# Two of four token sums on GpSimd, the other two a block of weights later, in an encoder layer on one Trainium2 core

## The chip, the cores and the metric

The kernel runs on one core of one Trainium2 chip. The core has TensorE (PE, matrix products into the accumulator memory PSUM; the loading of its weights, PEld, is shown apart), VectorE (DVE), ScalarE (ACT), GpSimd (POOL) and SyncE (SP, which here issues the DMAs), all of them working on the on-chip memory SBUF. Each engine takes its instructions in the order in which they were written and waits on semaphores for what the others produce. The metric is the device time of one execution in microseconds; lower is better.

## The reference

One encoder layer is applied to a prompt of 256 tokens and to a sample of 2048 tokens, all of width 1024, in float32. What matters here is its first step, the projection of the normalised tokens by one wide matrix:

```python
def encoder_layer(x, w_in, rpb, w_fourier, b_fourier, g_pre, g_na, g_f, w_out, g_post):
    h = rms_norm(x, g_pre)
    proj = h @ w_in
    q, k, v, z_a, u_f, z_f = jnp.split(proj, [...], axis=-1)
    y_a = neighbourhood_attention(q, k, v, rpb)
    y_f = fourier_mix(u_f, w_fourier, b_fourier)
    ...
    out = mixed @ w_out
    return x + rms_norm(out, g_post)
```

`w_in` is 1024 x 3072: six parts (q, k, v, z_a, u, z_f) of 512 columns. The attention, the Fourier mixing and the output product follow it in the kernel and are not touched by the change.

## The kernel before

**Products.** Float32 products are made of three products of a narrower kind: each operand is split into a high part and a low part, and `mm3` (lines 159 to 162) adds high x high (L160), and the two mixed products (L161, L162). The high part is a cast, made by ScalarE; the low part is "operand minus high part", made by VectorE. So each operand costs a ScalarE instruction and then a VectorE instruction that reads two SBUF tiles.

**The order of the first stages.** The kernel first makes v and u of the prompt and of part of the sample. Then comes a loop over 16 blocks `b` of 128 columns of weights (z_f, z_a, k, q, four blocks each), which makes these for the prompt's 256 tokens. After it, the function `vu` makes v and u of the first group of the sample's tokens (group 0; the sample's 2048 tokens are taken as two groups of 1024), and a long loop makes the other four parts for the group; then the same is done for group 1.

**Sums of token operands.** For the sample the products of a group are arranged in the manner of Strassen's multiplication: both matrices are cut into 2 x 2 parts, and seven products of sums of parts, the operands `j` = 0 to 6, take the place of eight. The four parts of group 0's tokens, `nq[kh, b]`, are tiles of 128 x 4 x 512 numbers (2048 per partition). They are loaded by `n_load`, scaled by VectorE in `n_scale` (L400), and combined by `n_sum` (L423), in this order:

- sum 0: t3 = (1,1) - (0,1), into a new tile
- sum 1: (0,1) = (0,1) - (0,0), in place
- sum 2: (0,0) = t3 + (0,0), in place
- sum 3: (1,0) = (0,0) - (1,0), in place, with the new (0,0)

`n_first(j)` then splits operand `j`: the cast on ScalarE (L428) and the low part on VectorE (L429). Operands 0 and 1 are the parts (0,0) and (1,0) before the sums; operand 2 is (0,0) after sum 2, operand 3 is (0,1) after sum 1, operand 4 is t3, operand 5 is (1,0) after sum 3.

**The loop over the blocks.** In this part of the program the order on all engines is written out by hand (`manual_schedule`). In the pass for block `b` the kernel issues, in this order: loads by SyncE; `b_raw(b + 2)`, which splits the weights of the block after the next (cast L562 or L565 on ScalarE, low part L563 or L566 on VectorE); a scaling (b = 2 to 7) or a sum (b = 8 to 11); `n_first` of operand 1, 2 or 3 (b = 5, 12, 13); from b = 14 on `op_split`, which splits the weights of group 0's first products (casts L477, low parts L478); then block `b`'s 24 products on TensorE, the evacuation of their PSUM tile by ScalarE (L789) and its store by SyncE (L791, L793).

So VectorE's queue holds, one behind the other: the low part of block 10, sum 0, block 11, sum 1, block 12, sum 2, block 13, sum 3, block 14, operand 2, block 15, operand 3, and then the low parts of the first weights of `vu`. Block `b` needs its low weights with its third product. The first product of `vu` needs the first L478 with its second.

**GpSimd** has nothing to do from the folding of u's weights (L265, in the first 30 us) to the sums of weights `w_sums` (L532), which are called within `vu`.

**The second group** does the same kind of work elsewhere: its operands come back from memory, and `b_split` (L439) splits them; there the low parts of operands 3 and 5 are made by GpSimd already.

## Time and profile before

| what | us |
|---|---|
| median of three runs | 966.51 |
| lowest and highest of them | 965.75, 966.55 |
| the profiled execution | 965.94 |
| its span, first to last instruction | 964.1 |
| TensorE busy in the span | 955.2 |
| VectorE busy | 703.4 |
| ScalarE busy | 496.7 |
| GpSimd busy | 427.0 |

The profile is of one execution. Its span reaches from the first to the last instruction; the rest of the execution's time lies around it. A row of the list in order of time gives the start, the duration, the engine, the line of the kernel, the operation, the tile written and the tiles read, the shape, a count where equal instructions were merged into one row, and in square brackets how long the engine had stood idle before and what released it. A row of the stage table gives a stretch of time, then the busy time of each engine in it with the number of its instructions, the clock that TensorE was granted (1.00 is full speed), and the load of the DMA engines.

### The profile page before, as it was taken

To read this page: it belongs to the slowest core of one execution; us is meant where nothing else is said; L and a number is where in the kernel's file an instruction comes from. 1 tells how busy PE (TensorE), PEld (TensorE's weight loads), DVE (VectorE), ACT (ScalarE), POOL (GpSimd) and SP (SyncE) were. 2 spreads that over 40 slices of the span, in tenths; PEclk is the share of its full clock that TensorE was granted. 3 is DMA by queue.
4 is the path that set the end of the run, shared out by engine and by line. 5 is a ranking of instruction groups with operands and counts; after the bars stand their busy time and mean duration, and the time that the engine had idled before them with its cause. 6 is when DMAs were issued, how large, how long until landed. Compare 5 with 4: busy or idle time off the path is not lost.

```text
span 964.1 us, 16993 instructions
## 1 busy us (share of the span) xinstructions
PE 955.2 (99%) x5743; PEld 799.0 (83%) x5743; DVE 703.4 (73%) x1310; ACT 496.7 (52%) x1077; POOL 427.0 (44%) x400
## 2 busy tenths in 40 slices
PE   9999999999999999999999999999999999999997
PEld 7889988888888888888888889888788887888886
DVE  5768978787876855687877458776765656659997
ACT  5845676423334532233344267677666676644443
POOL 2200002464751202674665043577677686524544
PEclk9999999999999999999999999999999999999999
DMA  8899796557848883499888896598877998979993
GB/s 304 317 354 380 248 348 243 199 203 263 298 185 345 299 347 123 181 362 360 308 294 327 306 335 225 169 285 292 258 235 238 287 285 286 301 253 346 332 353 122
DMA packets 140942, 269.81 MB, mean 280 GB/s; under 512 B 13402, under 2 KB 81840, under 8 KB 137464
## 3 DMA queue, kind: packets, MB, share of 16 engines
q1 hardware_dynamic: 140360, 268.32, 79.8%
q8 instruction: 46, 0.75, 0.3%
q10 hardware_dynamic: 432, 0.39, 0.2%
q14 instruction: 40, 0.33, 0.1%
q0 software_dynamic: 64, 0.02, 0.0%
HBM read 179.00 MB, written 96.81 MB: 286 GB/s over the span
## 4 chain that ended last, share of the span: by engine, by line
PE 96%; DVE 1%; DMA 1%; issue 0%; ACT 0%; DVEq 0%; SPq 0%; ACTq 0%
PE po L1454 20%; PE mm L161 18%; PE mm L160 18%; PE mm L162 18%; PE pv L1543 6%; PE ptb L1527 6%; PE s L1185 4%; PE pab L1022 2%; DMA wr<-wo 1%; PE py L160 1%; DMA gpre<-gpre 0%; PE py L162 0%; PE py L161 0%; PE ppq L1060 0%; PE pz L162 0%
## 5 line engine op out<-in xcount | busy, mean ns | idle before, releaser
L160 PE MATMUL mm<-xh,wa 128*128 128x512 f32 x448 | 174.4, 389 | 0.0
L162 PE MATMUL mm<-xh,wa 128*128 128x512 f32 x448 | 174.3, 389 | 0.0
L161 PE MATMUL mm<-xl,wa 128*128 128x512 f32 x448 | 174.3, 389 | 0.0
L532 POOL TENSOR_TENSOR ws<-wr 128x512 f32<-128x512 f32 x16 | 23.7, 1480 | 221.0 <-DVE vuo L505 123.8
L1219 POOL TENSOR_SCALAR w<-w,m 128x465 f32<-128x465 f32 (+9 forms) x136 | 84.7, 635 | 43.5 <-DVE m L1216 34.0
L162 PEld LDWEIGHTS mm<-xh,wa 128*128 128x128 f32 x448 | 84.1, 188 | 17.6
L160 PEld LDWEIGHTS mm<-xh,wa 128*128 128x128 f32 x448 | 84.1, 188 | 17.6
L161 PEld LDWEIGHTS mm<-xl,wa 128*128 128x128 f32 x448 | 84.1, 188 | 17.4
L1454 PE MATMUL po<-wo,yh 128*128 128x512 f32 x272 | 90.5, 414 | 0.0
L547 DVE TENSOR_TENSOR wa<-wr,wa 128x512 fp32r<-128x512 f32 x60 | 72.8, 1222 | 21.8 <-ACT wa L546 21.3
L1454 PE MATMUL po<-w,yh 128*128 128x512 f32 x280 | 86.8, 391 | 0.0
L1212 ACT ACTIVATE w<-w,m 128x465 f32<-128x465 f32 (+9 forms) x136 | 78.3, 579 | 13.3 <-DVE m L1207 12.9
L1207 DVE CUSTOM_DVE_ANT_1 w<-s,tb 128x465 f32<-128x465 f32 (+8 forms) x124 | 61.2, 531 | 9.8 <-PE s L1185 9.3
L161 PE MATMUL mm<-vl,xh 128*128 128x512 f32 x168 | 65.5, 390 | 0.2 <-DVE vl L478 0.2
L162 PE MATMUL mm<-vh,xl 128*128 128x512 f32 x168 | 65.4, 389 | 0.0
L160 PE MATMUL mm<-vh,xh 128*128 128x512 f32 x168 | 65.4, 389 | 0.0
L585 POOL TENSOR_TENSOR mt<-mt,rmask 128x880 f32<-128x880 f32 (+2 forms) x24 | 50.3, 2110 | 32.2 <-DVE mt L581 25.9
L1454 PEld LDWEIGHTS po<-w,yh 128*128 128x128 f32 x280 | 52.2, 188 | 10.9 <-issue 0.4
L1531 DVE COPY pt<-ptb 120x384 f32<-120x384 f32 (+5 forms) x72 | 40.5, 563 | 27.6 <-PE ptb L1527 27.4
L873 DVE TENSOR_TENSOR f<-u,mm 128x512 f32<-128x512 f32 x64 | 43.5, 679 | 22.3 <-PE mm L162 13.6
L546 ACT CAST wa<-wr 128x512 fp32r<-128x512 f32 x60 | 36.5, 618 | 44.7 <-PE mm L162 18.2
L1527 PE MATMUL ptb<-ident,w 128*120 128x128 f32 (+8 forms) x422 | 58.9, 276 | 0.0
(265 smaller groups left out, 2387.4 us busy)
## 6 DMA issues: line engine op xcount, KB each, us to landing
wr<-wz SPq DMA_DIRECT2D x48, 512.0 KB
vl<-sD SPq DMA_DIRECT2D x20, 512.0 KB
xm<-xm SPq DMA_DIRECT2D x9, 1024.0 KB
oD<-ofs SPq DMA_DIRECT2D x18, 512.0 KB
of<-oD SPq DMA_DIRECT2D x18, 512.0 KB
yr<-yD SPq DMA_DIRECT2D x34, 256.0 KB
zD<-f SPq DMA_DIRECT2D x16, 512.0 KB
xD<-nx SPq DMA_DIRECT2D x14, 512.0 KB
```

What stands on the lines that cost most here:

```text
L160: nc.tensor.matmul(out, lh, rh, start=first, stop=False)
L161: nc.tensor.matmul(out, lh, rl, start=False, stop=False)
L162: nc.tensor.matmul(out, ll, rh, start=False, stop=last)
L547: nc.vector.tensor_tensor(out=o[:, 1], in0=src, in1=o[:, 0].bitcast(F32), op=ALU.subtract)
L585: nc.gpsimd.tensor_tensor(out=o, in0=i, in1=rmask[:, m0:m0 + n].unsqueeze(2).to_broadcast([128, n, 80]), op=ALU.add)
L873: nc.vector.tensor_tensor(out=dst(f, b), in0=src(uu[u]), in1=src(p), op=op)
L1207: nc.vector.tensor_tensor_reduce(out=rows(g["w"][b][:, h, :n], w), in0=rows(g["s"][2 * b + h][:, :nr * sw(w)], sw(w))[:, :, :w], in1=tv, s ...
L1212: nc.scalar.activation(w, w, AF.Exp, bias=m[:, h:h + 1], scale=-1.0, accum_out=m[:, 2 + h:3 + h])
L1219: nc.gpsimd.tensor_scalar(w, w, m[:, 4 + h:5 + h], 1.0, ALU.mult, ALU.mult)
L1454: nc.tensor.matmul(p, (d["l"] if x == 2 else d["h"])[:, c], w(n, int(x == 1), c), start=j == 0, stop=j == 11)
L1527: nc.tensor.transpose(ptb[h][:nk, j * 128:j * 128 + 128], g["w"][b][:, h, c0:c0 + nk], ident)
L1543: nc.tensor.matmul(p[hs, b], g["v"][:nk, v, hs], g["pt"][b][:nk, h, j * 128:j * 128 + 128], start=j == 0, stop=j == len(ch) - 1)
```

## The change

Sums 0 and 3 are computed by GpSimd in place of VectorE. Sum 0 is still issued in block 8; sums 1, 2 and 3 are issued in blocks 10, 11 and 12, and no longer in 9, 10 and 11. Everything else stands in the same order. Semaphore waits between the two engines come with it: sum 1 overwrites a part that sum 0 reads, sum 2 reads t3, sum 3 reads what sum 2 wrote, and the splits of operands 4 and 5 read what GpSimd wrote.

```diff
@@ n_sum @@
         o, i0, i1, op = (("t3", (1, 1), (0, 1), ALU.subtract), ((0, 1), (0, 1), (0, 0), ALU.subtract),
                          ((0, 0), "t3", (0, 0), ALU.add), ((1, 0), (0, 0), (1, 0), ALU.subtract))[x]
-        nc.vector.tensor_tensor(out=nq[o], in0=nq[i0], in1=nq[i1], op=op)
+        (nc.vector if x in (1, 2) else nc.gpsimd).tensor_tensor(out=nq[o], in0=nq[i0], in1=nq[i1], op=op)
@@ the loop over the blocks @@
         if 2 <= b < 8:
             x, y = divmod(b, 2)
             n_scale(None, *divmod(x, 2)[::-1], range(2 * y, 2 * y + 2))
-        elif 8 <= b < 12:
-            n_sum(b - 8)
+        if b in (8, 10, 11, 12):
+            n_sum((8, 10, 11, 12).index(b))
         if b in (5, 12, 13):
             n_first((5, 12, 13).index(b) + 1)
```

## The prediction

> **What bounds the kernel now.** I read the page first (its parts 1 and 4), then the stage table of the stretch that the change touches, then VectorE (DVE), ScalarE (ACT) and the weight loads of TensorE (PEld) in order of time there, and last a place, 200 us later, where GpSimd (POOL) already does a sum of the size that is moved.

> ```profile
> span 964.1 us, 16993 instructions
> PE 955.2 (99%) x5743; PEld 799.0 (83%) x5743; DVE 703.4 (73%) x1310; ACT 496.7 (52%) x1077; POOL 427.0 (44%) x400
> PE 96%; DVE 1%; DMA 1%; issue 0%; ACT 0%; DVEq 0%; SPq 0%; ACTq 0%
> ```

> TensorE is busy 99% of the span and is 96% of the chain that ended last. So the rest of the kernel has nothing to give back: a microsecond that TensorE loses anywhere arrives at the end, and little can be won.

> ```profile
> core 0: us, PE busy (x) PEld busy (x) DVE busy (x) ACT busy (x) POOL busy (x), PEclk, DMA share, GB/s
> 98.60:123.00 24.40, 24.19 (x187) 23.18 (x186) 24.40 (x17) 16.95 (x21) 0.00 (x0) 1.00 0.68 230
> ```

> Here, where the four sums stand, it is different: VectorE is busy 24.40 of 24.40 us, GpSimd not at all. Its list in this stretch has no gap:

> ```profile
> 98.64 1.22 DVE L563 TENSOR_TENSOR wl<-wr,wh 128x1024 fp32r<-128x1024 f32 x1
> 99.78 2.28 DVE L423 TENSOR_TENSOR nt<-nx 128x2048 f32<-128x2048 f32 x1
> 101.98 1.22 DVE L563 TENSOR_TENSOR wl<-wr,wh 128x1024 fp32r<-128x1024 f32 x1
> 103.11 2.28 DVE L423 TENSOR_TENSOR nx<-nx 128x2048 f32<-128x2048 f32 x1
> 105.32 1.22 DVE L566 SCALAR_TENSOR_TENSOR wl<-wr,wh 128x1024 fp32r<-128x1024 f32 x1
> 106.45 2.28 DVE L423 TENSOR_TENSOR nx<-nt,nx 128x2048 f32<-128x2048 f32 x1
> 108.66 1.22 DVE L566 SCALAR_TENSOR_TENSOR wl<-wr,wh 128x1024 fp32r<-128x1024 f32 x1
> 109.79 2.28 DVE L423 TENSOR_TENSOR nx<-nx 128x2048 f32<-128x2048 f32 x1
> 111.99 1.22 DVE L566 SCALAR_TENSOR_TENSOR wl<-wr,wh 128x1024 fp32r<-128x1024 f32 x1
> 113.13 2.28 DVE L429 TENSOR_TENSOR xl<-nx,xh 128x2048 fp32r<-128x2048 f32 x1
> 115.33 1.22 DVE L566 SCALAR_TENSOR_TENSOR wl<-wr,wh 128x1024 fp32r<-128x1024 f32 x1
> 116.47 2.28 DVE L429 TENSOR_TENSOR xl<-nx,xh 128x2048 fp32r<-128x2048 f32 x1
> 118.67 4.62 DVE L478 TENSOR_TENSOR vl<-vr,vh 128x1024 fp32r<-128x1024 f32 x4
> ```

> The rows L563/L566 make the low parts of the weight blocks 10 to 15, the four L423 are the sums, the two L429 the low parts of token operands 2 and 3, L478 the first low part that the group's products need. From start to start a sum takes 2.20 us of this queue (99.78 to 101.98), a weight block 1.14, an L429 2.20.

> ```profile
> 104.73 0.19 PEld L161 LDWEIGHTS mm<-pl,wh 128*128 128x128 f32 x1
> 104.85 0.19 PEld L162 LDWEIGHTS mm<-ph,wl 128*128 128x128 f32 x1
> ...
> 116.25 0.19 PEld L161 LDWEIGHTS mm<-pl,wh 128*128 128x128 f32 x1
> 116.60 0.19 PEld L162 LDWEIGHTS mm<-ph,wl 128*128 128x128 f32 x1 [0.16 <-DVE wl L566]
> ...
> 119.94 0.19 PEld L161 LDWEIGHTS mm<-vl,xh 128*128 128x128 f32 x1 [0.52 <-DVE vl L478]
> ```

> The third product of a block (L162) is the first that reads the low weights. 116.60 is that of block 15, and 104.85 is four blocks earlier, block 11's: 116.25 - 104.73 = 11.52, so a block takes 2.88 us. VectorE is only just late today: TensorE waits 0.16 us for block 15 and 0.52 us for the group's first low part. These 0.7 us are all that taking work off VectorE can win here.

> **The change part by part.** Sums 0 and 3 leave VectorE for GpSimd; sums 1 and 2 stay and go one block later, to blocks 10 and 11; sum 3 is issued in block 12. No DMA is added or moved. Off VectorE's queue: 2 x 2.20 = -4.40 us. What a sum costs on GpSimd, and what it does to VectorE meanwhile, is shown at the second group's operands (L439), of the same 128x2048:

> ```profile
> 309.02 5.47 POOL L439 TENSOR_TENSOR xl<-xl,xh 128x2048 fp32r<-128x2048 f32 x1 [28.28 <-ACT xh L438]
> 318.26 5.14 POOL L439 TENSOR_TENSOR xl<-xl,xh 128x2048 fp32r<-128x2048 f32 x1 [3.77 <-ACT xh L438]
> ```

> ```profile
> 307.65 2.35 DVE L478 TENSOR_TENSOR vl<-vr,vh 128x1024 fp32r<-128x1024 f32 x2
> 309.93 0.68 DVE L873 TENSOR_TENSOR f<-u,mm 128x512 f32<-128x512 f32 x1
> 310.52 6.19 DVE L478 TENSOR_TENSOR vl<-vr,vh 128x1024 fp32r<-128x1024 f32 x2
> 316.63 2.28 DVE L439 TENSOR_TENSOR xl<-xl,xh 128x2048 fp32r<-128x2048 f32 x1
> 318.84 0.68 DVE L873 TENSOR_TENSOR f<-u,mm 128x512 f32<-128x512 f32 x1
> 321.93 3.62 DVE L439 TENSOR_TENSOR xl<-xl,xh 128x2048 fp32r<-128x2048 f32 x1 [2.42 <-ACT xh L438]
> ```

> The pair L478 takes 2.35 us at 307.65 and 6.19 us at 310.52, beside the GpSimd instruction: it got to run at 310.52 + 6.19 - 2.35 = 314.36. The last L439 takes 3.62 instead of 2.28: it ran at 323.27. Both are 0.13 us before GpSimd's end (314.49 and 323.40), and 4.36 us after the end of the VectorE instruction during which GpSimd had started (310.00, 318.91). So GpSimd waits for a running VectorE instruction that reads two SBUF tiles, and then such instructions wait for all of GpSimd's; L873, which reads a PSUM tile, runs through (0.68 both times). Everything in VectorE's list above reads two SBUF tiles. From the next free slot of VectorE's queue (0.08 before the end of the running instruction) the queue stands for 4.44 us per sum.

> [...]

> Now in order of time. Sum 0 needs only the last scaling before 98.64, so GpSimd starts in block 10's low part (98.64 to 99.86) and holds VectorE from 99.78 to 104.22. GpSimd's queue has nothing ahead of it and nothing behind it before 153 us:

> ```profile
> 153.21 1.81 POOL L532 TENSOR_TENSOR ws<-wr 128x512 f32<-128x512 f32 x1 [123.76 <-DVE vuo L505]
> ```

> ```profile
> 99.50 1.04 ACT L562 CAST wh<-wr 128x1024 fp32r<-128x1024 f32 x1
> ...
> 109.09 1.90 ACT L428 CAST xh<-nx 128x2048 fp32r<-128x2048 f32 x1
> ...
> 111.15 1.06 ACT L565 ACTIVATE wh<-wr 128x1024 fp32r<-128x1024 f32 x1
> ```

> Block 11's low part, whose cast ends at 100.54, waits at the head of VectorE's queue and runs 104.22 to 105.44 (now to 103.20). TensorE wants it at 104.85: a first stall of 0.6 us. Then, from 105.36 without a gap: block 12 (to 106.50), sum 1 (to 108.70; it overwrites what sum 0 read, but sum 0 is done), block 13 (109.84), sum 2 (112.04), block 14 (113.18). Sum 3 needs sum 2, so GpSimd asks at about 112.2 and gets its turn after block 14, in time for it: VectorE's next instruction, operand 2's low part, cannot be ready, since its cast (now at 109.09) also needs sum 2 and runs from 112.1 to 114.0. Behind that cast ScalarE's queue slips, with an evacuation of PSUM and block 15's cast (111.15 now, about 114.3 then), which is still ahead of VectorE. VectorE stands from 113.18 to 117.62; then operand 2 (to 119.82), block 15 (to 120.96, ended 121.04). TensorE, 0.6 us late, would want block 15's low part at about 117.0 and gets it at 121.1: a stall of 4.1 us. Operand 3 takes VectorE to 123.16, the first L478 ends at 124.38, and the group's first low-part product starts at 124.42 instead of 119.94. Behind it are the same instructions in the same order on all engines; stores and loads that SyncE issues behind ScalarE's evacuations slip by less than TensorE does.

> The sum: -2 x 2.20 + 2 x 4.44 = **+4.5 us** on VectorE's queue, which sets TensorE's start of the group; the 0.6 and 4.1 us of stall are this same delay as TensorE sees it (4.7, less 0.2 us of the waits there today). Moving sums 1 and 2 back costs nothing by itself: VectorE is just as full. Bounds of the unknown, the cost of a sum on GpSimd here: below, nothing of it stops VectorE, which would win the 0.7 us; above, the longest recorded length, 5.47, counted whole from the free slot, 1.03 more per sum, +6.5 us. I take 4.44, because two separate instances agree on it.

> The profiled execution took 965.94 us, 1.84 around its span, and 0.57 below the median of the three runs, 966.51. Put on the median: 966.5 + 4.5 = **971.0 us**.

> **The rivals.** *The clock falls during the stall.* TensorE's clock goes down when it rests:

> ```profile
> 956.90 0.28 PE L1742 MATMUL pl<-w,yl 128*128 128x128 f32 x1
> ```

> ```profile
> 961.50:962.00 0.50, 0.00 (x0) 0.00 (x0) 0.00 (x0) 0.00 (x0) 0.00 (x0) 0.59 1.03 377
> ```

> The last matmul ends at 957.18; the granted clock, a half at the end, averages 0.59 in that half microsecond, so it fell at about 961.6, after 4.4 us. The stall at block 15 is 4.1, less the last product's run. Close, but short of it. If it fell, block 15's 22 remaining products (0.12 us each, 2.64) would take up to twice as long, less 0.5 us that hide under the wait for L478: +2.1, 973.1 us. [...]

> *VectorE is not held up (the other side).* Were the sums on GpSimd to run beside VectorE's instructions, the queue would be 4.4 us shorter and both waits of today would go: 966.5 - 0.7 = 965.8. It turns on one number: below 2.20 us of blocking per sum the change wins, up to 3.2 us it stays within 0.2%. For it speaks only that GpSimd is free here; the rows at 310.52 and 321.93 are against it.

> *The delay is given back later.* If a later stage waited for DMA, TensorE could start late at no cost, and half or more of it would vanish: 968.5 or less. But TensorE is busy 99% of the span, and its order is fixed.

> **How the numbers follow.** Forecast (both sums block VectorE, clock stays up) 0.76, with its own range 970.0 to 972.0 (0.5 for the runs' spread and 0.25 per sum); clock falls or GpSimd takes its longest, 0.14; given back in part, 0.06; not held up, 0.04. The 8-in-10 range takes in the clock's fall: 969.3 to 973.2. About 0.2% (1.9 us) is what a measurement of this kernel can tell from no change. Slower by more: forecast, clock and half of "given back", 0.93. Within: 0.06. Faster by more: the best case wins only 0.7 us, so 0.01.

> **What would show it.** In the changed profile: two GpSimd rows L423 of about 5.2 us, from about 99 and 112; L563 after 100 and L429 after 114 on VectorE some 4 us too long; the weight loads of L162 waiting for L563 by about 0.6 us and for L566 by about 4; TensorE's busy time in 98.6 to 127.5 short by 4 to 5 us; everything behind shifted alike, with the granted clock at 1.00. The prediction fails if these VectorE rows keep 1.22 and 2.28 us, if sum 3 starts elsewhere, or if the granted clock dips behind 121 us.

## The result, and the profile after

The changed kernel takes 972.39 us (median of six runs, 971.50 to 975.33) beside 966.24 us (965.75 to 966.55) for the kernel before on the same chip. The ratio on record is 1.0069, with a 95% interval of 1.0056 to 1.0083: slower by 5.4 to 8.0 us. 971.0 was forecast.

The profiled execution is the fastest of the six, 971.50 us. Its page begins:

```profile
span 969.7 us, 16997 instructions
...
PE 956.0 (99%) x5743; PEld 800.1 (83%) x5743; DVE 710.0 (73%) x1308; ACT 496.6 (51%) x1077; POOL 439.7 (45%) x402
```

The span is 969.7 - 964.1 = 5.6 us longer. GpSimd has two instructions more and is 12.7 us busier. VectorE has two fewer and is 6.6 us busier all the same. These are the list of GpSimd and then that of VectorE where the sums stand:

```profile
98.47 5.41 POOL L423 TENSOR_TENSOR nt<-nx 128x2048 f32<-128x2048 f32 x1 [68.92 <-DMA wr<-wz]
111.78 5.50 POOL L423 TENSOR_TENSOR nx<-nx 128x2048 f32<-128x2048 f32 x1 [7.89 <-DVE nx L423]
```

```profile
98.17 1.22 DVE L563 TENSOR_TENSOR wl<-wr,wh 128x1024 fp32r<-128x1024 f32 x1
100.10 4.87 DVE L563 TENSOR_TENSOR wl<-wr,wh 128x1024 fp32r<-128x1024 f32 x1 [0.71 <-ACT wh L562]
104.89 1.21 DVE L566 SCALAR_TENSOR_TENSOR wl<-wr,wh 128x1024 fp32r<-128x1024 f32 x1
106.03 2.28 DVE L423 TENSOR_TENSOR nx<-nx 128x2048 f32<-128x2048 f32 x1
108.23 1.21 DVE L566 SCALAR_TENSOR_TENSOR wl<-wr,wh 128x1024 fp32r<-128x1024 f32 x1
109.36 2.28 DVE L423 TENSOR_TENSOR nx<-nt,nx 128x2048 f32<-128x2048 f32 x1
111.57 1.21 DVE L566 SCALAR_TENSOR_TENSOR wl<-wr,wh 128x1024 fp32r<-128x1024 f32 x1
113.62 5.80 DVE L429 TENSOR_TENSOR xl<-nx,xh 128x2048 fp32r<-128x2048 f32 x1 [0.84 <-ACT xh L428]
119.35 1.21 DVE L566 SCALAR_TENSOR_TENSOR wl<-wr,wh 128x1024 fp32r<-128x1024 f32 x1
120.48 2.28 DVE L429 TENSOR_TENSOR xl<-nx,xh 128x2048 fp32r<-128x2048 f32 x1
122.68 2.35 DVE L478 TENSOR_TENSOR vl<-vr,vh 128x1024 fp32r<-128x1024 f32 x2
```

Two of VectorE's instructions are far too long. Block 11's low part (100.10) takes 4.87 us instead of 1.22, and operand 2's (113.62) 5.80 instead of 2.28. They got to run only when GpSimd's sums were ending: the sums end at 103.88 and 117.28, and the two instructions got to run at 100.10 + 4.87 - 1.22 = 103.75 and 113.62 + 5.80 - 2.28 = 117.14, which is 0.13 and 0.14 us before. All others keep their length. This execution reached the first row 0.47 us earlier than the one before did (98.17 against 98.64); counted from there, the first L478 starts 122.68 - 118.67 + 0.47 = 4.48 us later.

What TensorE sees of it, as weight loads and as matmuls, in order of time:

```profile
105.02 0.19 PEld L162 LDWEIGHTS mm<-ph,wl 128*128 128x128 f32 x1 [0.57 <-DVE wl L563]
120.61 0.19 PEld L162 LDWEIGHTS mm<-ph,wl 128*128 128x128 f32 x1 [4.01 <-DVE wl L566]
```

```profile
116.52 0.28 PE L161 MATMUL mm<-pl,wh 128*128 128x256 f32 x1
120.61 0.39 PE L162 MATMUL mm<-ph,wl 128*128 128x256 f32 x1 [3.81 <-DVE wl L566]
...
121.02 0.42 PE L161 MATMUL mm<-pl,wh 128*128 128x256 f32 x1
121.23 0.41 PE L162 MATMUL mm<-ph,wl 128*128 128x256 f32 x1
121.44 0.41 PE L160 MATMUL mm<-ph,wh 128*128 128x256 f32 x1
...
125.07 0.40 PE L161 MATMUL mm<-vl,xh 128*128 128x512 f32 x1
```

Block 11 waits 0.57 us for its low weights, block 15 waits 4.01. The group's first low-part product starts at 125.07, where it was 119.94: 5.13 + 0.47 = 5.60 us later, and so 1.12 us more than VectorE's queue explains. The rows after the rest say why: the products of block 15 follow one another in 0.21 us (121.02, 121.23, 121.44), while those of the blocks before take 0.12. The stage table, whose last columns are the granted clock, the DMA share and GB/s, shows the clock:

```profile
core 0: us, PE busy (x) PEld busy (x) DVE busy (x) ACT busy (x) POOL busy (x), PEclk, DMA share, GB/s
98.60:123.00 24.40, 20.22 (x159) 19.82 (x158) 22.85 (x11) 14.68 (x18) 10.78 (x2) 0.96 0.59 206
117.45:120.86 3.41, 0.25 (x2) 0.25 (x3) 3.41 (x3) 3.41 (x5) 0.00 (x0) 1.00 0.23 77
120.86:124.27 3.41, 3.41 (x18) 3.41 (x18) 3.41 (x3) 0.07 (x1) 0.00 (x0) 0.50 0.00 0
124.50:130.00 5.50, 5.50 (x28) 4.60 (x27) 5.09 (x4) 2.78 (x3) 0.00 (x0) 1.00 0.59 163
```

In the rest itself it is still 1.00, from 120.86 to 124.27 it is 0.50, then 1.00 again. From there to the end nothing is given back: counted from the span's start the shift is 5.13 us at the group's first low-part product and 5.6 at the end. In between, TensorE waits 0.9 us for one tile of VectorE's (L1294) where it waited 0.2 before; why this wait is longer is not shown.

### The profile page after: what moved, and what is told of

Its sections match the earlier page's. It is cut to its first block, busy times and chain, and to the rows that moved or that the text cites. A ratio compares the mean times of both kernels' runs of the same rounds, so it can differ in the third digit from the quotient of the medians.

```text
span 969.7 us, 16997 instructions
## 1 busy us (share of the span) xinstructions
PE 956.0 (99%) x5743; PEld 800.1 (83%) x5743; DVE 710.0 (73%) x1308; ACT 496.6 (51%) x1077; POOL 439.7 (45%) x402
## 4 chain that ended last, share of the span: by engine, by line
PE 96%; DVE 1%; issue 1%; DMA 0%; ACT 0%; DVEq 0%; SPq 0%; ACTq 0%
PE po L1454 20%; PE mm L162 18%; PE mm L161 18%; PE mm L160 18%; PE pv L1543 6%; PE ptb L1527 6%; PE s L1185 4%; PE pab L1022 2%; PE py L160 1%; PE py L162 1%; PE py L161 1%; DVE nx L423 0%; DMA gpre<-gpre 0%; PE ppq L1060 0%; PE pz L161 0%
## 5 line engine op out<-in xcount | busy, mean ns | idle before, releaser
L162 PE MATMUL mm<-xh,wa 128*128 128x512 f32 x448 | 174.3, 389 | 0.0
L161 PE MATMUL mm<-xl,wa 128*128 128x512 f32 x448 | 174.3, 389 | 0.0
L161 PEld LDWEIGHTS mm<-xl,wa 128*128 128x128 f32 x448 | 84.1, 188 | 17.4
L162 PEld LDWEIGHTS mm<-xh,wa 128*128 128x128 f32 x448 | 84.1, 188 | 17.4
L532 POOL TENSOR_TENSOR ws<-wr 128x512 f32<-128x512 f32 x16 | 24.2, 1514 | 138.9 <-DMA wr<-wz 126.3
L162 PE MATMUL mm<-vh,xl 128*128 128x512 f32 x168 | 65.4, 389 | 0.0
L161 PE MATMUL mm<-vl,xh 128*128 128x512 f32 x168 | 65.4, 389 | 0.0
L873 DVE TENSOR_TENSOR f<-u,mm 128x512 f32<-128x512 f32 x64 | 43.5, 679 | 21.9 <-PE mm L162 16.5
```

The source lines that it names most:

```text
L161: nc.tensor.matmul(out, lh, rl, start=False, stop=False)
L162: nc.tensor.matmul(out, ll, rh, start=False, stop=last)
L873: nc.vector.tensor_tensor(out=dst(f, b), in0=src(uu[u]), in1=src(p), op=op)
```

## The experiments

Each ratio, with its interval, is the one on record, against runs of the kernel before on the same chip; it is not the quotient of the two medians, and differs from it by up to 0.0014. Diffs are against the changed kernel unless it is said otherwise. "The first L478" is given relative to the first row of VectorE's list, as above.

**All four sums on VectorE, at the changed places.** This keeps the moves of sums 1, 2 and 3 and takes GpSimd out.

```diff
-        (nc.vector if x in (1, 2) else nc.gpsimd).tensor_tensor(out=nq[o], in0=nq[i0], in1=nq[i1], op=op)
+        nc.vector.tensor_tensor(out=nq[o], in0=nq[i0], in1=nq[i1], op=op)
```

> The four sums stand where the changed kernel has them (blocks 8, 10, 11, 12), but all are made by VectorE. Theory (GpSimd's sums block VectorE): VectorE's queue is as long as before, only in another order; block 15's low part and the first L478 end as before, TensorE waits 0.2 and 0.5 us: 966.2 us, within 0.5. Rival (the later places of the sums, and ScalarE's cast of operand 2 waiting for the late sum 2, make the loss): most of it stays, about 970 us, with VectorE idle in front of L429.

Measured: 966.54 us, ratio 0.9994 (0.9985 to 1.0002). The first L478 is 0.30 us later, and TensorE's waits, in the view of waits (total, times, longest), are small:

```profile
PE mm L162 <- DVE wl L566: 0.3, 1, 0.3
PE mm L161 <- DVE vl L478: 0.2, 1, 0.2
```

So the later places cost nothing that can be measured. The loss comes from the engine that does the sums.

**One sum at a time on GpSimd.** First sum 0 alone:

```diff
-        (nc.vector if x in (1, 2) else nc.gpsimd).tensor_tensor(out=nq[o], in0=nq[i0], in1=nq[i1], op=op)
+        (nc.vector if x else nc.gpsimd).tensor_tensor(out=nq[o], in0=nq[i0], in1=nq[i1], op=op)
```

> Sum 0 alone on GpSimd, in block 8; sums 1 to 3 on VectorE in blocks 10 to 12. Theory: one sum off VectorE (-2.20), one block of 4.44: the first L478 2.2 us later; TensorE waits 0.6 us for block 11 and about 1.8 for block 15, too short for the clock to fall: 966.2 + 2.2 = 968.5 us, granted clock as before. Rival (any sum on GpSimd is free unless something waits for its result): 964 to 966.5, since sum 0's result is wanted only three blocks later. Rival (the clock falls in any stall): 969.5 or more, clock under 0.999.

Then sum 3 alone:

```diff
-        (nc.vector if x in (1, 2) else nc.gpsimd).tensor_tensor(out=nq[o], in0=nq[i0], in1=nq[i1], op=op)
+        (nc.vector if x < 3 else nc.gpsimd).tensor_tensor(out=nq[o], in0=nq[i0], in1=nq[i1], op=op)
```

> Sum 3 alone on GpSimd, in block 12; sums 0 to 2 on VectorE in blocks 8, 10 and 11. Theory: the same +2.2 us on VectorE's queue, all of it as one stall of about 2.4 us in front of block 15's third product; no clock fall: 968.5 us. If a rest of about 2.4 us already lowers the clock: 969.5 or more, with rows of 0.50 after the stall. If GpSimd's sum is free: 965.5 to 966.5.

Measured: sum 0 alone 968.64 us, ratio 1.0021 (1.0012 to 1.0031); sum 3 alone 969.30 us, ratio 1.0027 (1.0016 to 1.0038). VectorE's rows of the first kernel, and then of the second:

```profile
98.63 1.22 DVE L563 TENSOR_TENSOR wl<-wr,wh 128x1024 fp32r<-128x1024 f32 x1
100.56 4.87 DVE L563 TENSOR_TENSOR wl<-wr,wh 128x1024 fp32r<-128x1024 f32 x1 [0.71 <-ACT wh L562]
...
120.90 1.21 DVE L478 TENSOR_TENSOR vl<-vr,vh 128x1024 fp32r<-128x1024 f32 x1
```

```profile
111.51 5.80 DVE L429 TENSOR_TENSOR xl<-nx,xh 128x2048 fp32r<-128x2048 f32 x1 [0.84 <-ACT xh L428]
...
120.57 2.35 DVE L478 TENSOR_TENSOR vl<-vr,vh 128x1024 fp32r<-128x1024 f32 x2
```

Each sum alone makes the same long instruction as in the changed kernel, and no other. The first L478 is 120.90 - 118.67 + 0.01 = 2.24 us later with sum 0. With sum 3 it is 120.57 - 118.67 + 0.65 = 2.55 later (the first row is at 97.99 there), which is 2.24 and the 0.30 of the places. So a sum costs 4.44 - 2.20 = 2.24 us, and the two simply add up. In these two profiles block 15 rests 1.6 and 2.5 us and the clock stays at 1.00. But the runs with sum 3 fall into two kinds, 4 of 967.3 to 967.7 us and 8 of 969.0 to 971.3. A fall of the clock in part of them would explain some of that: four of the eight (969.5 to 971.3) have a mean granted clock of 0.996 on record, where the kernel before has 0.997 to 0.999 beside them. The profiled run, 969.10, is one of the other four and shows no fall.

**Is it the clock?** Two kernels fill part of block 15's rest with products of ones whose result is not used. The first has 8 of them:

```diff
+        if b == 15:
+            fill = ps.tile([128, 512], F32, tag="c", name="fill", bufs=1)
+            for x in range(8):
+                nc.tensor.matmul(fill[:, :128], onesq, onesq, start=True, stop=True)
```

> The changed kernel, with eight matmuls of ones on a tile that nobody reads in front of block 15's products, so that TensorE rests about 2 us there and not 4. Theory (1.0 us and more of the loss is the clock, which fell to 0.50 from 121.0 to 124.3 in the stall's wake): the stall ends at the same time, the clock stays at 1.00, and the time is 966.2 + 4.5 = 970.7 us, with less spread between runs than the changed kernel's 971.5 to 975.3. Rival (the clock has no part; TensorE waits for the low parts of the group's weights either way, or the rest is lost later): 972.4 us as it is.

Measured: 972.76 us, ratio 1.0053 (1.0036 to 1.0069). One row of TensorE, and one of the stage table:

```profile
120.52 0.39 PE L162 MATMUL mm<-ph,wl 128*128 128x256 f32 x1 [2.02 <-DVE wl L566]
```

```profile
121.60:125.00 3.40, 3.40 (x18) 3.30 (x17) 3.40 (x4) 0.17 (x1) 0.00 (x0) 0.50 0.03 5
```

The rest is halved, to 2.0 us, and the clock falls all the same, to a half for 3.4 us. The group's first low-part product is 5.57 us later than before, 1.1 more than VectorE's queue explains, as in the changed kernel. The expectation failed: I had thought that a rest of half the length was safe. The second kernel differs in one number:

```diff
-            for x in range(8):
+            for x in range(17):
```

> The changed kernel with 17 matmuls of ones in front of block 15 in place of eight. Eight left a rest of 2.0 us and the clock fell all the same; 17 take about 3.6 us and leave a rest of about 0.4 us. Theory (what is above 4.5 us of the loss is the fallen clock): granted clock 1.00 throughout 110 to 130 us, time 966.2 + 4.5 = 970.7 us, 1 to 2 us below the changed kernel beside it. Rival (the clock has no part in the time): the same as the changed kernel.

With it ran the changed kernel once more, unaltered:

> The changed kernel once more, beside the others on the same chip. Theory: stall of about 4 us in front of block 15's third product, clock at 0.50 for some 3.4 us behind it, 971.5 to 973.5 us. If the clock stays up in this execution: 970.7 us.

Measured: 971.12 us with 17, ratio 1.0045 (1.003 to 1.006); the changed kernel again 973.05 us, ratio 1.0070 (1.0053 to 1.0088). The stage table of the one, then of the other:

```profile
115.00:130.00 15.00, 14.78 (x104) 13.46 (x103) 14.99 (x8) 10.09 (x12) 3.65 (x1) 1.00 0.32 101
```

```profile
119.50:126.40 6.90, 5.64 (x24) 5.53 (x25) 6.90 (x7) 2.08 (x4) 0.00 (x0) 0.51 0.06 19
```

With no rest longer than 0.5 us the clock stays at 1.00, and the group's first low-part product comes 4.47 us later than before, which is VectorE's queue and nothing else. In the repeated run the clock is down for 6.8 us, twice 3.4, and that product comes 6.4 us later. So the changed kernel loses about 4.5 us to VectorE's queue, and on top of it a clock term: 1.1 us in the first profile, 1.9 in the second, and 973.05 - 971.12 = 1.9 between the medians of these two kernels (six runs each, which spread over some 3 us, so that this difference is rough).

The traces also show when the clock falls. In each of the twelve profiles it changes only at points that lie whole multiples of 3.413 us apart: in the changed kernel's it is at 1.00 for 34 such stretches, at 0.50 for one and at 1.00 for 247. These are the stretches around the rest with 8 products, and then those with sum 3 alone:

```profile
118.18:121.60 3.42, 1.40 (x12) 1.20 (x11) 3.42 (x3) 2.66 (x4) 0.00 (x0) 1.00 0.11 38
```

```profile
114.13:117.54 3.41, 1.87 (x16) 1.66 (x14) 3.41 (x2) 3.41 (x6) 1.03 (x1) 1.00 0.11 38
117.54:120.96 3.42, 2.46 (x20) 2.46 (x21) 3.42 (x3) 1.28 (x2) 0.00 (x0) 1.00 0.11 38
```

The rest of 2.0 us lies within one stretch, of which TensorE is busy for 1.40 us, and the clock falls at its end. The longer rest of 2.5 us lies across an edge, and the clock stays. Over all full stretches at 1.00 in the twelve profiles, the clock fell after each with 1.76 us of TensorE's work or less and after none with 2.12 or more; between them it stayed after 1.82, 1.85 and 1.87 and fell after 1.99. The edges lie elsewhere in each execution: a rest of 2.0 us was followed by a fall in one profile, and one of 2.5 us by none in another. In the repeated run the stretch behind the fall holds 2.23 us of work (119.58 to 122.99) and the clock stays down; the next one is full, and the clock comes back at its end.

**Sum 3 out of the full stretch.** Both kernels put sum 3 behind the group's second product; the first has all sums on VectorE. Its diff is against the kernel before:

```diff
-        elif 8 <= b < 12:
+        elif 8 <= b < 11:
             n_sum(b - 8)
...
+    at(1, n_sum, 3)
```

> The kernel before, all sums on VectorE, sum 3 moved out of block 11 into the second product of the group, where VectorE had idle time (1.6 us at 125.4). Theory (VectorE's full queue sets the start of the group): 2.2 us come off its queue ahead of it, the waits of 0.2 and 0.5 us go, nothing new comes: 965.5 us, 0.7 below before, at the edge of what can be measured. If the waits come back at the group's evacuations: 966.2.

The second is the same with sum 3 on GpSimd:

```diff
-        nc.vector.tensor_tensor(out=nq[o], in0=nq[i0], in1=nq[i1], op=op)
+        (nc.vector if x < 3 else nc.gpsimd).tensor_tensor(out=nq[o], in0=nq[i0], in1=nq[i1], op=op)
```

> As e6_late, but sum 3 on GpSimd. Theory: GpSimd's queue is empty, so sum 3 starts as soon as sum 2 is done (about 109), wherever it stands in the program, and blocks VectorE for 4.4 us there: 2.2 us longer than on VectorE, 968.4 us. Rival (the later place in the program moves it into VectorE's idle time): 965.5 us, as e6_late.

Measured: 965.11 us on VectorE, ratio 0.9994 (0.9983 to 1.0005); 969.28 us on GpSimd, ratio 1.0033 (1.0022 to 1.0045). On VectorE TensorE waits nowhere any more for a low part of these weights; all of its waits are:

```profile
PE idle L225 <- POOL onesq L221: 1.0, 1, 1.0
PE mm L160 <- ACT xh L284: 0.3, 1, 0.3
```

The waits of 0.16 and 0.52 us of the kernel before are gone, and there is no more to win here; the interval takes in no change. On GpSimd the sum did not run late. Rows of GpSimd, VectorE, TensorE and the stage table:

```profile
108.23 6.65 POOL L423 TENSOR_TENSOR nx<-nx 128x2048 f32<-128x2048 f32 x1 [79.57 <-DMA vr<-wv]
```

```profile
108.01 2.35 DVE L566 SCALAR_TENSOR_TENSOR wl<-wr,wh 128x1024 fp32r<-128x1024 f32 x2
110.37 6.65 DVE L429 TENSOR_TENSOR xl<-nx,xh 128x2048 fp32r<-128x2048 f32 x1
```

```profile
118.22 0.39 PE L162 MATMUL mm<-ph,wl 128*128 128x256 f32 x1 [2.21 <-DVE wl L566]
```

```profile
119.10:122.40 3.30, 3.30 (x17) 3.30 (x17) 3.30 (x3) 0.00 (x0) 0.00 (x0) 0.50 0.00 0
```

GpSimd's queue is empty, so the sum runs as soon as sum 2 is done, wherever it stands in the program, and operand 2's low part waits for it: 6.65 us instead of 2.28. The first L478 is 2.26 us later, as for one sum at any place of the full stretch. And a rest of 2.2 us is followed by a fall of the clock here too.

**What on GpSimd holds VectorE?** Both kernels have all sums on VectorE, and additional work on GpSimd whose result is not used. The first has a tiny sum and then ten memsets of a 128x512 tile, which only write:

```diff
-        (nc.vector if x in (1, 2) else nc.gpsimd).tensor_tensor(out=nq[o], in0=nq[i0], in1=nq[i1], op=op)
+        nc.vector.tensor_tensor(out=nq[o], in0=nq[i0], in1=nq[i1], op=op)
...
+    scr = hp.tile([128, 512], F32, name="scr")
...
+        if b == 8:
+            nc.gpsimd.tensor_tensor(out=scr[:, :1], in0=nq[1, 1][:, 3, :1], in1=nq[0, 1][:, 3, :1], op=ALU.add)
+            for x in range(10):
+                nc.gpsimd.memset(scr, 0.0)
```

> All sums on VectorE in the places of the changed kernel (e1_order), and beside them in block 8, released by the last scaling, ten fills of a scratch tile (128x512) by GpSimd, some 5 us that write SBUF and read nothing; a 128x1 sum in front of them sets their time. The scratch tile is read by nobody. Theory (VectorE waits for GpSimd's reading of SBUF): the VectorE rows keep 1.22 and 2.28 us, 966.5 us as e1_order. Rival (any GpSimd instruction that uses SBUF holds VectorE): L563 and L423 in 99 to 104 us grow by 4 to 5 us together, about 970.5 us.

The second has, in place of these, four sums of 128x512 each, together as large as sum 0:

```diff
+        if b == 8:
+            for x in range(4):
+                nc.gpsimd.tensor_tensor(out=scr, in0=nq[1, 1][:, x], in1=nq[0, 1][:, x], op=ALU.add)
```

> As e9_memset, with four extra sums of 128x512 into the scratch tile in place of the fills: the same reading of SBUF as one 128x2048 sum, but nothing is taken off VectorE, and VectorE may run between the pieces. Theory: VectorE's rows in 99 to 107 us grow by 4 x 1.1 = 4.4 us together, the first L478 comes about 4.4 us later than in e1_order, 966.5 + 4.4 = 970.9 us, and up to 2 us more where the clock falls. Rival (a sum on GpSimd harms only by being awaited): as e1_order.

Measured: 966.14 us with the memsets, ratio 0.9998 (0.9990 to 1.0007); 969.99 us with the additional sums, ratio 1.0039 (1.0026 to 1.0052). Lines of `n_sum` are one higher here (L424). GpSimd and VectorE with the memsets:

```profile
98.79 4.44 POOL L775 TENSOR_TENSOR scr<-nx 128x1 f32<-128x1 f32 x1 [68.14 <-DVE nx L401]
103.29 5.78 POOL L777 MEMSET scr<- 128x512 f32 x10
```

```profile
103.40 1.23 DVE L567 SCALAR_TENSOR_TENSOR wl<-wr,wh 128x1024 fp32r<-128x1024 f32 x1 [0.22 <-ACT wh L566]
104.54 2.29 DVE L424 TENSOR_TENSOR nx<-nx 128x2048 f32<-128x2048 f32 x1
```

GpSimd writes SBUF from 103.29 to 109.07, and VectorE's instructions beside it keep 1.23 and 2.29 us. Busy with memsets, GpSimd did not hold VectorE. (Whether it is a sum's reading of SBUF that does, these runs do not separate from the rest of what a sum does.) And with the additional sums:

```profile
95.29 8.50 POOL L776 TENSOR_TENSOR scr<-nx 128x512 f32<-128x512 f32 x4 [65.06 <-DVE nx L401]
```

```profile
96.93 3.48 DVE L401 SCALAR_TENSOR_TENSOR nx<-nx,gpre,iv 128x512 f32<-128x512 f32 x2
100.34 2.31 DVE L564 TENSOR_TENSOR wl<-wr,wh 128x1024 fp32r<-128x1024 f32 x1
102.57 3.38 DVE L424 TENSOR_TENSOR nt<-nx 128x2048 f32<-128x2048 f32 x1
```

These take 1.41, 1.22 and 2.28 us elsewhere: together 2.07 + 1.09 + 1.10 = 4.3 us more, for a sum's worth of GpSimd work from which VectorE gains nothing. This measures the hold by itself, and it is close to what one whole sum holds, 4.44. The first low part of the group's weights comes 4.28 us later than in the kernel before and 3.97 later than with all sums on VectorE at these places, both counted from the weight block at 93.33, since the later rows are held up themselves; 4.4 was expected, and the median is 3.7 above the kernel before, not 4.4. (The pieces began earlier than I had meant, since the first of them need only the earlier scalings.)

## Why the prediction was right, and where it was not

The measured 972.39 us lies in the range of 969.3 to 973.2, but above the forecast's own 970.0 to 972.0: it is in the range because that was made to take in a fall of the clock, to which a small chance was given.

- **The forecast's own mechanism held, to the hundredth.** Delay of the first L478: 2 x (4.44 - 2.20) = 4.48 us forecast, 4.48 measured. GpSimd's end after that of the running VectorE instruction: 4.49 and 4.50 (103.88 - 99.39, 117.28 - 112.78), where 4.49 was read beforehand. VectorE's turn 0.13 and 0.14 before GpSimd's end, where it was 0.13 at 200 us further on. Stalls of TensorE: 0.6 and 4.1 forecast, 0.57 and 4.01 measured. One sum costs 2.24 us alone, and the same work added without taking anything off VectorE costs VectorE 4.3. Taking a sum off VectorE saves 2.20 and adds 4.44.
- **"Moving sums 1 and 2 back costs nothing by itself": right.** 0.30 us in the order of VectorE's queue, nothing that the time shows (0.9994).
- **The slip on ScalarE and block 15's cast: right.** It started at 113.76, or 114.23 with the 0.47, where about 114.3 was forecast.
- **"VectorE is not held up": wrong**, as judged from the rows of the kernel before at 310.52 and 321.93. The instructions at 100.10 and 113.62 took 4.87 and 5.80 us instead of 1.22 and 2.28, and the delay of 4.48 us is that of 4.44 us of hold for a sum. The runs show the hold and its length, not what in the chip makes it.
- **"The delay is given back later": wrong.** The shift is 5.1 us at the group's first low-part product and 5.6 at the end of the span.
- **The step that failed is "Close, but short of it": that the clock stays up.** The forecast held that a rest of 4.1 us, less the last product's run, ends before the clock falls, because at the end of the kernel the fall came 4.4 us after the last matmul, and gave the fall, together with GpSimd's longest time, a chance of 0.14. The clock fell in both profiles of the changed kernel, from 120.86 us in the first; a dip behind 121 us was one of the prediction's own signs of failing. The sum lacked a term of 1.1 us (first profile) to 1.9 us (second profile, with two stretches at 0.50, and the medians with and without the rest). With it, 966.2 + 4.5 + 1.1 to 1.9 = 971.8 to 972.6, where the two medians are 972.39 and 973.05. The rival itself had the mechanism and the place right and priced it at +2.1, with all 22 remaining products of block 15 at half the clock. The fall lasted 3.41 us in the first profile; half of that, less the 0.5 us that hide under the wait for L478, is an estimated 1.2, close to the 1.1 measured. One reading of a delay at another place was no bound: rests of 2.0 and 2.2 us were enough for a fall elsewhere, and the fall at the end of the kernel comes 1.4 to 4.6 us after the last matmul in the twelve profiles. The 4.4 of the kernel before is set by where its edges lie, as the last two stretches in front of its fall show:

```profile
954.76:958.18 3.42, 2.42 (x19) 2.27 (x17) 3.18 (x10) 1.68 (x7) 3.22 (x3) 1.00 0.12 45
958.18:961.59 3.41, 0.00 (x0) 0.00 (x0) 2.55 (x6) 0.46 (x2) 0.57 (x1) 1.00 0.53 201
```

A rest of 3.8 us puts at least 1.9 us of it into one stretch, wherever the edges lie, which leaves 1.5 us of work or less. After every such stretch in these profiles the clock fell, so by this estimate a fall was to be expected here in nearly every execution.

What stays open: what decides on a fall where a stretch holds between 1.8 and 2.0 us of work, as this busy time alone does not. And one run of the changed kernel took 975.33 us, 9.1 above the kernel before; 4.5 and 1.9 leave 2.7 of it. It is not the profiled one, so this is not explained; single runs of the kernel before lie as far above their median (968.98 beside 966.24).

## What to carry to other kernels

Before giving an idle engine work, look at which instructions of the full engine it will meet: here a GpSimd sum of two SBUF tiles stopped VectorE for 4.44 us to save it 2.20, while memsets on GpSimd cost nothing that could be measured. Such a price could be read beforehand at a place of the trace where the two engines already met: an instruction of a known shape that took far longer than elsewhere (in the kernel before the pair L478 at 310.52, 6.19 us instead of 2.35). A wait of TensorE of 2 us or more should be priced with a possible fall of the clock behind it (1.1 us here, or 1.9 where it lasted for two stretches), and not only with its own length.
